# Sixteen more first products per layer, made beside the gate build and kept in DRAM

## The chip, the cores and the metric

The kernel runs on one core of one Trainium2 chip. The metric is device time in microseconds (us) of one execution; the time before is 4202.59 us, the median of three runs (4202.59 to 4206.1).

## The reference, cut to what matters

The model has two layers over 768 tokens (256 of a context, 512 latent) of width 1024. Each layer has a mixer (attention and the like) and then a PEER block: a router picks, for each token and each of 8 heads, 16 out of 16384 single-neuron experts. For a token `x`, the block gives the sum over its 128 picked experts of `gate * gelu(x . u[e]) * v[e]`:

```python
eidx = jnp.take_along_axis(cidx.reshape(n, PEER_HEADS, -1), ci, axis=-1)
gate = jax.nn.softmax(cs, axis=-1)
a = jnp.einsum('nd,nhkd->nhk', xt, u[eidx])
w = gate * jax.nn.gelu(a, approximate=False)
return jnp.einsum('nhk,nhkd->nd', w, v[eidx])
```

The second layer needs only the latent tokens.

## The kernel before, in words

**Dense and gathered tokens.** Of the 512 latent tokens of a layer, three blocks of 128 (`ND` = 384 tokens) are done densely: all 16384 experts are computed for them, and a matrix of gates that is zero for the experts not picked takes out the rest. The fourth block (and in the first layer the two context blocks) is done by gathering: one indirect DMA fetches one row of `u` or `v` for each of 128 tokens, VectorE multiplies it up. Such a step is called a row here (`gather`, L1010 to L1036). The rows are spread over other work by hand: 272 of the first layer's 768 lie in the mixer, 78 beside the gate build, 64 in the next mixer and the others in the dense loop; all 256 of the second layer lie in its dense loop.

**The order in one layer's `peer`.**

1. `route`: `scores` makes 16 query products (`pqps`) with weights that come through the buffers `wraw` (three), `whi` and `wlo` (two each) and the PSUM tag `pj` (two). Then `select` picks the experts of each block, nearly all on VectorE.
2. `gate_build`, once per dense block after that block's selection: 32 units per block, 96 per layer. A unit makes gates for four tokens: two matmuls `gds` (L1091), one VectorE operation (L1095) and one of ScalarE (L1097) on their result, then four fp32 matmuls `gps` (L1108, eight recorded pieces). Every second unit has a ScalarE copy to `gch`; every fourth stores 1 MB to `gd` in DRAM. `beside(hot)` is called once in each unit and places gathered rows, queued on VectorE behind the unit's L1095 (`issue_after` orders instructions of that one engine and no other's).
3. In the first layer only, `mod(1, [0, 1])`: 16 weight tiles through `wraw`, with results in `pj`.
4. The first products that are made early: for the first `UPRE` = 18 (second layer 27) groups of 128 experts, `dense_u` makes `z[j] = u_j . x` for 384 tokens. The weight tile (512 KB) comes through `wraw`, ScalarE casts it to `whi` (L195), GpSimd and VectorE in turn subtract to `wlo` (L196), 24 matmuls of 384 columns (L217) go to a `pj` tile, ScalarE copies to `z`.
5. The dense loop over 128 groups. Iteration `j` makes the first product of group `j + ahead` (24 matmuls L217; `ahead` is 21 and 28; weight tile `draw`, ScalarE cast L1122, GpSimd subtract L1123), turns `z[j+1]` into `w[j+1]` (`dense_w`: VectorE multiplies by the gates in L1168, ScalarE casts in L1171, VectorE subtracts in L1172), loads the second weight tile of group `j`, and adds its 18 matmuls of 512 columns (`dacc`, L1178). The `z` tiles form a ring of `ahead + 1` buffers. Rows are placed behind each iteration's L1172.

**What sets the order on each engine.** The order of each engine's instructions is fixed when the program is built, by a scheduler that plays the program against a model of its time. It takes, among the instructions that could start, the one that is written first; an instruction of a later step may go ahead as long as what is written earlier is not ready. A tile gets a buffer of its tag when one is free, and a tile that finds none waits. Loads of weights are issued on SP's queue.

Of the kernel before, what the change touches and what calls it, by code (L numbers as in the profile page):

```python
# [9 lines left out]
F32 = mybir.dt.float32  # L10
# [12 lines left out]
ND = 384  # L23
# [5 lines left out]
GROWS = 78, 0  # L29
# [2 lines left out]
NLAT = 5  # L32
FIRST = 1, 1, 0, 1, 0, 1, 0, 1, 0, 1, 0, 1, 1, 0, 0, 0
XA, VPRE = 2, 2
UEXT = 3, 1
TAIL = 4
GEND = 124
# [73 lines left out]
class Kern:  # L111
    def __init__(self, ctx, tc, a, dbg=None):
        self.ctx, self.tc, self.nc, self.a = ctx, tc, tc.nc, a
        self.dbg = dbg or {}
        E = ctx.enter_context
        self.pc = E(tc.tile_pool(name="cst", bufs=1, reuse_waits="tile"))
        self.pg = E(tc.tile_pool(name="gat", bufs=1, reuse_waits="tile"))
        self.px = self.xt = E(tc.tile_pool(name="xt", bufs=1, reuse_waits="tile"))
        self.dr = E(tc.tile_pool(name="dr", bufs=1, space=bass.MemoryType.DRAM))
        self.wk = None  # L120
        nc = self.nc
        self.tables()
        self.cst = self.pc.tile([128, CST_N], F32, name="cst")
        self.ident = self.c("ident")
        self.eps = self.pc.tile([128, 1], F32, name="eps")
        nc.vector.memset(self.eps, EPS)
        self.one = self.c("ones")[:, 0:1]
        self.modd = self.dr.tile([2, 2, 6 * D], F32, name="modd")
        self.hd = self.dr.tile([768, D], F32, name="hd")
        self.x2d = self.dr.tile([768, D], F32, name="x2d")  # L130
        self.h1 = self.dr.tile([768, D], F32, name="h1")
        self.gd = self.dr.tile([ND // 16, 128, 128, 16], F32, name="gd")
        self.yd = self.dr.tile([2, D, 768], F32, name="yd")
        self.bd = self.dr.tile([ND // 128, 1024, 256], BF16, name="bd")

    def consts(self):
# [979 lines left out]
    def halves(self, src, shape, eng):  # L1116
# [6 lines left out]
        eng.tensor_tensor(lo, raw, hi.bitcast(F32), op=OP.subtract)  # L1123
        return hi, lo

    def dense_u(self, j, u, A, xt):


        nc = self.nc
        self.proj2(A, u, xt, ND)  # L1130
        if j % (self.ahead + 1) <= self.upre:
            z = self.dz.tile([128, ND], F32, name="dz", tag="dz", bufs=self.upre + 1)
        else:
            z = self.dn.tile([128, ND], F32, name="dz", tag="dze", bufs=self.ahead - self.upre)
        if j < self.ahead:
            nc.scalar.copy(z, A)
        else:
            nc.scalar.activation(z, A, AF.Gelu)  # L1138
        return z
# [3 lines left out]
        return self.halves(self.a["pr_v"][r:r + 128, :], [D], self.nc.vector)  # L1143

    def ahead_u(self, l, n, pda, xt, z, eng):
        u = self.halves(self.a["uT"][l, n], [8, 128], eng)
        A = pda.tile([128, ND], F32, name="dA", tag="dA", bufs=2)
        z[n] = self.dense_u(n, u, A, xt)
# [10 lines left out]
    def dense_w(self, j, z):  # L1159
        nc = self.nc  # L1160
        JG = self.jg
        if j > 0 and j % JG == 0:
            self.load_gates(j, range(3))
        if j < self.ahead:
            with self.tc.issue_after(self.lastexp.ins):
                nc.scalar.activation(z, z, AF.Gelu)
        z3 = z.rearrange("p (c t) -> p c t", t=16)
        nc.vector.tensor_tensor(z3, z3, self.G[:, :, j % JG, :], op=OP.mult)  # L1168
        wh, wl = (self.dn.tile([128, ND], F32R, name="dw", tag="dw" + x, bufs=2) if j < 128 - TAIL else
                  self.dz.tile([128, ND], F32R, name="dw", tag="dz", bufs=self.upre + 1) for x in "hl")  # L1170
        nc.scalar.copy(wh, z)  # L1171
        i = nc.vector.tensor_tensor(wl, z, wh.bitcast(F32), op=OP.subtract)  # L1172
        return wh, wl, i
# [166 lines left out]
    def peer(self, l, xt, bb, gat, rows, done, late, put):  # L1340

        tc, nc = self.tc, self.nc
        PS = bass.MemoryType.PSUM
        nd = ND // 128
        nb = 4
        upre = self.upre = UPRE[l]
        self.ahead = upre + UEXT[l]
        self.jg = JGS[l]  # L1350
        with tc.tile_pool(name="dz", bufs=1, reuse_waits="tile") as self.dz:
            with self.mixing(), self.phase("rt"):
                pool, tag = ((self.wk, "sel"), (self.pg, "uv"))[l]
                alloc = lambda: pool.tile([128, D], F32, name="sel", tag=tag, bufs=5)
                self.gate_consts()
                step = [0]

                def beside(hot):

                    step[0] += 1  # L1360
                    if step[0] * GROWS[l] // 96 > (step[0] - 1) * GROWS[l] // 96:
                        with tc.issue_after(hot.ins):
                            next(rows)

                sel = self.route(l, xt, nb, nd, alloc, lambda *a: self.gate_build(*a, beside))
                if l == 0:
                    self.mod(1, [0, 1])
                z = {}
                for j in range(upre):
                    u = self.parts(self.weight(self.a["uT"][l, j], [128, 8, 128]), (nc.gpsimd, nc.vector)[j % 2])  # L1370
                    z[j] = self.dense_u(j, u, self.pj([128, ND], "dA"), xt)
            gat += [(bb + b, LAT, sel[b]) for b in range(nd, nb)]
            left, done = 256 * len(gat) - done - GROWS[l] - late, 0
            with tc.tile_pool(name="dn", bufs=1, reuse_waits="tile") as self.dn, \
                    tc.tile_pool(name="pda", bufs=1, space=PS, reuse_waits="tile") as pda, \
                    self.phase("d2"), tc.tile_pool(name="pd", bufs=1, space=PS, reuse_waits="tile") as pd:
                acc = [pd.tile([128, 2, 512], F32, name="dacc%d" % b) for b in range(nd)]
                self.load_gates(0, [0, 1])
                for n in range(upre, self.ahead):
                    self.ahead_u(l, n, pda, xt, z, (nc.gpsimd, nc.vector)[(n - upre) % XA])  # L1380
                vs = {n: self.v_rows(l, n) for n in range(VPRE)}
                self.load_gates(0, [2])
                w = {0: self.dense_w(0, z.pop(0))}
                last = []
                for j in range(128):
                    if j + self.ahead < 128:
                        self.ahead_u(l, j + self.ahead, pda, xt, z, nc.gpsimd)
                    if j == TJ:
                        self.tables(True)
                    if j + 1 < 128:  # L1390
                        w[j + 1] = self.dense_w(j + 1, z.pop(j + 1))
                    wj = w.pop(j)
                    v = vs.pop(j) if j in vs else self.v_rows(l, j)
                    if j < 128 - TAIL:
                        for b in range(nd):
                            self.dense_v(j, b, wj, v, acc)
                    else:
                        last.append((j, wj, v))
                    with tc.issue_after(wj[2].ins):
                        while done < min(left * (j + 2) // GEND, left):  # L1400
                            next(rows)
                            done += 1
                for b in range(nd):
                    for j, wj, v in last:
                        self.dense_v(j, b, wj, v, acc)
                m5 = self.row5(l, LAT)
                for b in range(nd):
                    put(bb + b, self.resid(m5, acc[b].rearrange("p h d -> p (h d)"), bb + b))
# [139 lines left out]
```

## Time and profile before

| | before |
| --- | --- |
| median of the runs shown | 4202.59 us |
| the profiled execution: its time, and its span | 4207.51 us, 4205.7 us |
| PE busy, PE weight loads busy | 3816.9 us (91%), 3259.6 us (78%) |
| VectorE (DVE) busy | 3316.6 us (79%) |
| ScalarE (ACT) busy | 1508.1 us (36%) |
| GpSimd (POOL) busy | 2261.8 us (54%) |
| mean granted clock of TensorE | 0.955 |

Times inside the profile count from the first instruction. The first layer's selection and gate build lie at about 1086 to 1390 us and its dense loop at about 1419 to 2400 us; the second layer's at about 2966 to 3240 us and 3247 to 4195 us. A busy time of PE is that of pipelined matmuls whose ends are modelled, so two views of it are needed: how often a matmul starts, and what lies in the gaps.

### The profile page before, as it was taken

How to read it: one execution, taken by the hardware profiler on the slowest of the kernel's cores; microseconds unless marked ns; L12 is line 12 of the kernel's file. 1: busy time of each engine (PE TensorE's matmuls, PEld its weight loads, DVE VectorE, ACT ScalarE, POOL GpSimd, SP SyncE). 2: the span in 40 equal slices, each digit the busy share in tenths (PEclk: the TensorE clock that was granted, in tenths of full speed). 3: DMA queues.
4: the chain of work that ended last, by engine and by line, in shares of the span. 5: the costliest groups of instructions: out<-in, count | busy, mean ns of one | idle time of the engine just before them, and what ended most of it. 6: DMA issues, size and time to landing. Idle time of an engine off the chain costs nothing.

```text
span 4205.7 us, 56328 instructions
## 1 busy us (share of the span) xinstructions
PE 3816.9 (91%) x19774; PEld 3259.6 (78%) x19780; DVE 3316.6 (79%) x5835; ACT 1508.1 (36%) x2746; POOL 2261.8 (54%) x1644
## 2 busy tenths in 40 slices
PE   8988776769888799999999889999989999999999
PEld 5776554547777699988999767777877899999987
DVE  4359888866998899989999987537875977777788
ACT  3322322312146333333333324332356333333333
POOL 1016777542454587877888563004531666666664
PEclk9999888879999999999999999999999999999999
DMA  5556898783449999999999995423346988787878
GB/s 192 172 200 209 308 322 307 253 287 121 149 161 398 367 332 334 332 324 333 346 339 331 341 333 194 158 85 111 111 160 235 346 279 285 275 290 273 282 268 313
DMA packets 389674, 1099.30 MB, mean 261 GB/s; under 512 B 32959, under 2 KB 140807, under 8 KB 383246
## 3 DMA queue, kind: packets, MB, share of 16 engines
q0 software_dynamic: 147456, 536.94, 35.2%
q1 hardware_dynamic: 232142, 497.95, 34.6%
q10 hardware_dynamic: 9792, 60.82, 3.5%
q8 instruction: 155, 2.54, 0.2%
q14 instruction: 129, 1.06, 0.1%
HBM read 1024.18 MB, written 71.40 MB: 260 GB/s over the span
## 4 chain that ended last, share of the span: by engine, by line
PE 58%; DVE 16%; DMA 11%; issue 8%; POOL 6%; ACT 2%; SPq 0%; ACTq 0%; POOLq 0%; DVEq 0%
PE dacc L1178 20%; PE dA L217 18%; POOL uv L1010 4%; DMA uv<-in_pr_u_dram,ix 3%; PE ops L223 3%; DMA uv<-in_pr_v_dram,ix 3%; PE pqps L217 2%; DVE junkv L1023 2%; PE gps L1108 2%; DMA draw<-in_uT_dram 1%; PE oo L1335 1%; DVE pacc L1036 1%; PE gds L1091 1%; PE modps L252 1%; PE oqps L210 1%
## 5 line engine op out<-in xcount | busy, mean ns | idle before, releaser
L1178 PE MATMUL dacc<-dhi,dw 128*128 128x512 f32 x3072 | 983.7, 390 | 3.4 <-ACT dw L1171 1.9
L1010 POOL DMA_INDIRECT uv<-in_pr_u_dram,ix x512 | 669.4, 1307 | 447.7 <-DVE pa L1023 316.0
L1010 POOL DMA_INDIRECT uv<-in_pr_v_dram,ix x512 | 680.0, 1328 | 408.0 <-DVE pacc L1036 281.9
L1023 DVE CUSTOM_DVE_ANT_0 junkv<-uv,x 128x1024 bf16<-128x1024 f32 x512 | 692.6, 1353 | 65.0 <-DMA uv<-in_pr_u_dram,ix 60.9
L1036 DVE SCALAR_TENSOR_TENSOR pacc<-uv,pw,pacc 128x1024 f32<-128x1024 f32 x508 | 701.5, 1381 | 39.3 <-DMA uv<-in_pr_v_dram,ix 35.4
L1178 PEld LDWEIGHTS dacc<-dhi,dw 128*128 128x128 f32 x3072 | 576.5, 188 | 119.5 <-ACT dw L1171 2.2
L1123 POOL TENSOR_TENSOR dlo<-draw,dhi 128x1024 fp32r<-128x1024 f32 x210 | 545.0, 2596 | 194.9 <-ACT dhi L1122 191.4
L1122 ACT CAST dhi<-draw 128x1024 fp32r<-128x1024 f32 x467 | 489.0, 1050 | 404.9 <-issue 179.5
L1178 PE MATMUL dacc<-dlo,dw 128*128 128x512 f32 x1536 | 601.6, 392 | 5.2 <-DVE dlo L1123 5.2
L1168 DVE TENSOR_TENSOR dz<-dz,dG 128x384 f32<-128x384 f32 x256 | 416.9, 1642 | 73.6 <-ACT dz L1138 71.8
L1171 ACT CAST dw<-dz 128x384 fp32r<-128x384 f32 x256 | 131.5, 514 | 721.2 <-PE dacc L1178 694.3
L1123 DVE TENSOR_TENSOR dlo<-draw,dhi 128x1024 fp32r<-128x1024 f32 x257 | 331.9, 1292 | 17.7 <-ACT dhi L1122 16.1
L217 PE MATMUL dA<-xth,dlo 128*128 128x384 f32 x1688 | 328.1, 335 | 19.0 <-POOL dlo L1123 19.0
L217 PE MATMUL dA<-xth,dhi 128*128 128x384 f32 x1688 | 334.6, 340 | 5.1 <-ACT dhi L1122 5.1
L1178 PEld LDWEIGHTS dacc<-dlo,dw 128*128 128x128 f32 x1536 | 288.2, 188 | 63.8 <-DVE dlo L1123 7.6
L217 PE MATMUL dA<-xtl,dhi 128*128 128x384 f32 x1688 | 326.9, 334 | 0.0
L217 PEld LDWEIGHTS dA<-xth,dhi 128*128 128x128 f32 x1688 | 305.7, 189 | 21.6 <-ACT dhi L1122 5.5
L217 PEld LDWEIGHTS dA<-xth,dlo 128*128 128x128 f32 x1688 | 296.5, 188 | 20.0 <-POOL dlo L1123 20.0
L217 PEld LDWEIGHTS dA<-xtl,dhi 128*128 128x128 f32 x1688 | 296.4, 188 | 0.0
L1172 DVE TENSOR_TENSOR dw<-dz,dw 128x384 fp32r<-128x384 f32 x256 | 154.4, 603 | 150.3 <-ACT dw L1171 150.3
L196 POOL TENSOR_TENSOR wlo<-wraw,whi 128x1024 fp32r<-128x1024 f32 x55 | 132.8, 2416 | 246.7 <-ACT whi L195 129.6
L1108 PEld LDWEIGHTS gps<-ghot 128*128 128x128 f32 x1536 | 205.0, 195 | 70.7 <-issue 39.0
(339 smaller groups left out, 6072.2 us busy)
## 6 DMA issues: line engine op xcount, KB each, us to landing
draw<-in_pr_v_dram SPq DMA_DIRECT2D x256, 512.0 KB
draw<-in_uT_dram SPq DMA_DIRECT2D x211, 512.0 KB
wraw<-in_wb_dram SPq DMA_DIRECT2D x150, 512.0 KB
gd<-gch ACTq DMA_DIRECT2D x48, 1024.0 KB
dG<-gd SPq DMA_DIRECT2D x30, 1536.0 KB
wraw<-in_mod_t_dram SPq DMA_DIRECT2D x48, 512.0 KB
wraw<-in_uT_dram SPq DMA_DIRECT2D x45, 512.0 KB
wraw<-in_mod_w_dram SPq DMA_DIRECT2D x32, 512.0 KB
```

What stands on the lines that cost most here:

```text
L196: eng.tensor_tensor(lo, raw, hi.bitcast(F32), op=OP.subtract)
L217: self.nc.tensor.matmul(ps, w[wi][:, k, :], x[xi][:, k, 0:T], start=(i == 0), stop=(i == 23))
L1010: nc.gpsimd.indirect_dma_start(out=t, out_offset=None, in_=a[table], in_offset=bass.IndirectOffsetOnAxis(ap=ix[:, c:c + 1], axis=0))
L1023: nc.vector.tensor_tensor_reduce(out=junk, in0=u, in1=x, op0=OP.mult, op1=OP.add, scale=1.0, scalar=0.0, accum_out=A[:, c:c + 1])
L1036: nc.vector.scalar_tensor_tensor(acc, v, W[:, c:c + 1], acc, op0=OP.mult, op1=OP.add)
L1108: nc.tensor.matmul(ps[0][:, t0 % 8 + t, :], h[0][:, t, :], h[1][:, t, :], start=True, stop=True)
L1122: nc.scalar.copy(hi, raw)
L1123: eng.tensor_tensor(lo, raw, hi.bitcast(F32), op=OP.subtract)
L1168: nc.vector.tensor_tensor(z3, z3, self.G[:, :, j % JG, :], op=OP.mult)
L1171: nc.scalar.copy(wh, z)
L1172: i = nc.vector.tensor_tensor(wl, z, wh.bitcast(F32), op=OP.subtract)
L1178: self.nc.tensor.matmul(acc[b][:, h, :], w[wi][:, 128 * b:128 * b + 128], v[vi][:, 512 * h:512 * h + 512], start=(j == 0 and i == 0), stop ...
```

## The change

In each layer, the first products of 16 more groups of experts are taken out of the dense loop. The list `spill` names them: they are spread evenly over the groups from `ahead` on. Each is made by a new function `store_u(k)`, called from `beside` at every fifth unit of the gate build from the 21st on (units 21, 26, ..., 96): weight tile through `wraw`, cast, subtract (on GpSimd in the first layer, on VectorE in the second), 24 matmuls into a `pj` tile, a VectorE copy to SBUF, and a store of 192 KB to the new DRAM tile `zd`. In the dense loop, a spilled group loads its 192 KB from `zd` into its `z` tile on SP's queue in place of the 512 KB weight tile, the cast, the subtract, the 24 matmuls and the evacuation; its Gelu, before part of the evacuation, is taken from the tile in `dense_w`. The 78 gathered rows beside the first layer's gate build lie beside units 17 to 96 now, before beside all 96.

```diff
 XA, VPRE = 2, 2
+USP = 16, 16
 UEXT = 3, 1
...
+        self.zd = self.dr.tile([2, max(USP), 128, ND], F32, name="zd")
...
+    def z_tile(self, j):
+        if j % (self.ahead + 1) <= self.upre:
+            return self.dz.tile([128, ND], F32, name="dz", tag="dz", bufs=self.upre + 1)
+        return self.dn.tile([128, ND], F32, name="dz", tag="dze", bufs=self.ahead - self.upre)
...
     def ahead_u(self, l, n, pda, xt, z, eng):
+        if n in self.spill:
+            z[n] = self.z_tile(n)
+            self.nc.sync.dma_start(z[n], self.zd[l, self.spill.index(n)])
+            return
...
-        if j < self.ahead:
+        if j < self.ahead or j in self.spill:
             with self.tc.issue_after(self.lastexp.ins):
                 nc.scalar.activation(z, z, AF.Gelu)
...
+        self.spill = [self.ahead + (127 - self.ahead) * k // USP[l] for k in range(USP[l])]
...
+                def store_u(k):
+                    u = self.parts(self.weight(self.a["uT"][l, self.spill[k]], [128, 8, 128]),
+                                   (nc.gpsimd, nc.vector)[l])
+                    A = self.pj([128, ND], "dA")
+                    self.proj2(A, u, xt, ND)
+                    t = self.wk.tile([128, ND], F32, name="zs", tag="pq", bufs=2)
+                    nc.vector.tensor_copy(t, A)
+                    nc.sync.dma_start(self.zd[l, k], t)
+
                 def beside(hot):
                     step[0] += 1
-                    if step[0] * GROWS[l] // 96 > (step[0] - 1) * GROWS[l] // 96:
+                    u = step[0] - 16
+                    if u > 0 and u * GROWS[l] // 80 > (u - 1) * GROWS[l] // 80:
                         with tc.issue_after(hot.ins):
                             next(rows)
+                    if u > 0 and u * USP[l] // 80 > (u - 1) * USP[l] // 80:
+                        with tc.issue_after(hot.ins):
+                            store_u((u - 1) * USP[l] // 80)
```

## Rows read from the trace of the kernel before

**Rows 1.** The page: granted clock of TensorE in forty slices of the span.
```profile
PE   8988776769888799999999889999989999999999
PEclk9999888879999999999999999999999999999999
```
**Rows 2.** Busy time of each engine in the two dense loops (us, in brackets instructions).
```profile
core 0: us, PE busy (x) PEld busy (x) DVE busy (x) ACT busy (x) POOL busy (x), PEclk, DMA share, GB/s
1440.00:2376.00 936.00, 930.53 (x4664) 841.07 (x4663) 869.82 (x846) 340.95 (x458) 728.77 (x435) 1.00 0.93 334
...
3262.00:4150.00 888.00, 886.32 (x4434) 800.41 (x4433) 716.38 (x720) 322.24 (x433) 581.92 (x336) 1.00 0.83 292
```
**Rows 3.** Timeline of one second-layer iteration: start, duration, engine, line.
```profile
3607.37 1.48 PEld L217 LDWEIGHTS dA<-xth,dhi 128*128 128x128 f32 x8
...
3611.61 0.19 PEld L1178 LDWEIGHTS dacc<-dhi,dw 128*128 128x128 f32 x1
...
3615.68 1.48 PEld L217 LDWEIGHTS dA<-xth,dhi 128*128 128x128 f32 x8
```
**Rows 4.** The second layer's gate build by windows: early units, then the others.
```profile
3030.00:3112.00 82.00, 71.77 (x401) 66.89 (x401) 75.56 (x219) 39.43 (x69) 45.27 (x43) 0.92 0.32 109
3112.00:3240.00 128.00, 121.84 (x850) 99.04 (x851) 58.12 (x84) 92.05 (x133) 2.15 (x4) 1.00 0.58 221
```
**Rows 5.** Timeline of two units of that gate build.
```profile
3150.21 1.08 PEld L1108 LDWEIGHTS gps<-ghot 128*128 128x128 f32 x8
...
3151.37 0.76 PE L1091 MATMUL gds<-gB,gbits 128*128 128x512 bf16 x2
3151.76 1.07 PEld L1108 LDWEIGHTS gps<-ghot 128*128 128x128 f32 x8 [0.29 <-issue]
...
3152.86 0.59 PE L1091 MATMUL gds<-gB,gbits 128*128 128x512 bf16 x2
...
3153.08 1.08 PEld L1108 LDWEIGHTS gps<-ghot 128*128 128x128 f32 x8
```
**Rows 6.** The first layer: selection, gate build, start of the dense loop.
```profile
1086.00:1150.00 64.00, 54.54 (x402) 44.96 (x401) 56.85 (x241) 10.93 (x16) 27.70 (x22) 1.00 0.51 174
1150.00:1390.00 240.00, 202.34 (x1269) 170.32 (x1271) 216.38 (x488) 129.57 (x195) 114.14 (x117) 0.96 0.77 291
```
**Rows 7.** Early first products in the first and second layer: PE, PEld, ACT on `dA`.
```profile
1086.00:1150.00 64.00, 21.71 (x125) 21.71 (x126) 2.40 (x5) 1.00 0.51 174
1150.00:1254.00 104.00, 60.75 (x309) 55.27 (x307) 6.19 (x13) 0.90 0.45 156
...
2966.00:3030.00 64.00, 58.31 (x324) 57.33 (x323) 6.22 (x13) 0.97 0.36 119
3030.00:3112.00 82.00, 61.00 (x289) 55.31 (x289) 5.69 (x12) 0.92 0.32 109
3112.00:3240.00 128.00, 0.25 (x2) 0.20 (x2) 0.48 (x1) 1.00 0.58 221
```
**Rows 8.** SP's queue after the scores: weight loads of steps 3 and 4, first layer.
```profile
1063.37 0.33 SPq L250 DMA_DIRECT2D wraw<-in_mod_t_dram  x1
...
1121.63 0.35 SPq L250 DMA_DIRECT2D wraw<-in_mod_t_dram  x1
...
1122.39 1.69 SPq L187 DMA_DIRECT2D wraw<-in_uT_dram  x2
...
1150.06 0.33 SPq L1077 DMA_DIRECT2D bd<-sel  x1
```
**Rows 9.** SP's queue in the second layer, to the first unit's loads.
```profile
2943.99 77.29 SPq L187 DMA_DIRECT2D wraw<-in_uT_dram  x16
3021.95 0.33 SPq L1077 DMA_DIRECT2D bd<-sel  x1
3027.14 0.93 SPq L1088 DMA_DIRECT2D gbits<-bd  x2
```
**Rows 10.** PE's timeline where the two dense loops start (in brackets idle, releaser).
```profile
1385.07 2.17 PE L1108 MATMUL gps<-ghot 128*128 128x128 f32 x16
1389.78 2.93 PE L217 MATMUL dA<-xth,dhi 128*128 128x384 f32 x8 [2.54 <-ACT dhi L1122]
...
1413.60 2.93 PE L217 MATMUL dA<-xth,dlo 128*128 128x384 f32 x8 [17.91 <-POOL dlo L1123]
...
1419.04 0.39 PE L1178 MATMUL dacc<-dhi,dw 128*128 128x512 f32 x1
...
3236.10 1.16 PE L1108 MATMUL gps<-ghot 128*128 128x128 f32 x8 [0.28 <-ACT ghot L1097]
...
3247.44 0.50 PE L1178 MATMUL dacc<-dhi,dw 128*128 128x512 f32 x1 [1.88 <-ACT dw L1171]
```
**Rows 11.** First-layer dense loop: L1168 by duration (min, median, max in ns).
```profile
L1168 DVE TENSOR_TENSOR dz<-dz,dG x97: 543/2374/3000, 1499.6 to 2299.4; 128x384 f32<-128x384 f32 x97
```
**Rows 12.** SP's queue in the second dense loop: what its longest waits are for.
```profile
SPq L1119 <- DVE dlo L1123: 282.6, 70, 4.6
SPq L1119 <- POOL dlo L1123: 190.9, 63, 4.0
```

More of the change, by code (lines that the diff above doesn't have):

```diff
@@ L1130, in dense_u @@
         self.proj2(A, u, xt, ND)
[L1131 to L1134, printed above, removed]
+        z = self.z_tile(j)
         if j < self.ahead:
```

## The prediction

> **What bounds the kernel now.** I read the page first, then the windows of each stage, then the timeline inside a stage. The page says PE, VectorE and at times the DMA queues are all near full, and the granted clock is near the upper of its two levels (2.4 GHz) nearly everywhere [rows 1]; so what a stage is worth is read stage by stage. In both dense loops PE is busy in 99% to 100% of the window [rows 2]. In the second layer nothing else is near full (VectorE 716 of 888 us, DMA share 0.83). In the first layer VectorE has 870 of 936 us and the DMA share is 0.93: a faster PE meets them soon. One iteration shows PE's price [rows 3]: 24 weight loads of a first product run from 3607.37 to 3611.61, 4.24 us, the second product to 3615.68, 4.07 us, sum 8.31 us, with no gap.
>
> The gate build is the place to which the products go. In the second layer PE is busy 121.8 of 128 us there, with VectorE at 58 us and ScalarE at 92 us [rows 4]; two units take 2.87 us (3150.21 to 3153.08), 1.435 us each, and the only pause is one of 0.29 us per pair [rows 5]. In the first layer the gate build shares its time with selection and rows: VectorE 216 of 240 us, PE 202 [rows 6].
>
> The last reading decides the forecast: what PE does before the gate units are ready. Selection is VectorE's work, and PE fills that time with step 4's early products, which are written after the gate build but are ready sooner. From 2966 to 3030 us they take 58.3 of 64 us, to 3112 another 61.0 of 82, and then none is left [rows 7]. In the first layer PE makes step 3 and then step 4 in this time (54.5 of 64 us busy, then 60.8 us of products to 1254) [rows 6, 7].
>
> **The change part by part.** *Taken out of the dense loops:* 16 first products per layer, 16 x 4.24 = 68 us of PE each [rows 3]. In the second layer PE is the only bound, so all 68 us come back. In the first layer PE would need 930.5 - 68 = 863 us for the window. VectorE keeps its instructions; some get shorter, since L1168 takes 543 ns alone and 2374 ns in the median [rows 11], which I put down to GpSimd's subtract running beside it, and 16 of those go: 16 x 1.83 = 29 us, so 841 us of work. At 95% fullness (93% now [rows 2]) that is 885 us. DMA: 16 x (512 - 192) KB = 5 MB less of some 313 MB, 0.93 x 936 = 870 us becomes about 856 us of full queues. I take 885, a gain of 51 us; bounds 25 us (no shorter instructions and 93% to 96% fullness) and 68 us.
>
> *The loads of `z`* wait for a buffer of the ring that `dense_w` frees, and SP's later loads queue behind them. SP's ordinary waits there, for a `draw` buffer, reach 4.6 us without PE noticing [rows 12, 2], and the ring buffer needed is that of two iterations earlier; I take nothing, with a rival below. The Gelu is moved, not added. ScalarE loses a cast; it is busy 36% of these windows [rows 2].
>
> *Put into the gate build:* 16 x 4.24 = 68 us of PE per layer, and on VectorE a copy that no row shows; its nearest neighbour is the 0.69 us operation on 512 columns of PSUM (L1095) in the unit, so 0.3 to 0.69 us, taken as 0.5: 8 us per layer, on a VectorE that is at 90% in the first layer and 45% in the second [rows 4, 6]. In the second layer the subtracts add some 20 us to a VectorE that has 70 us free [rows 4]. Stores and loads of 192 KB are 3 MB a layer, 10 us of DMA at 291 GB/s [rows 6], hidden where the DMA share is under 0.8. The pauses of PE (0.29 us per pair, some 12 us over 85 units) could take a little of the 68; I take nothing.
>
> *What it moves.* `store_u` is written before steps 3 and 4 and needs the same buffers: `wraw`, `whi`, `wlo`, `pj`. Only its VectorE instructions are queued behind a unit; its weight load, cast and matmuls are not. So right after the scores the first three `store_u` take the three `wraw` buffers, two take `whi` and `pj`, and they hold them: a `pj` tile is freed by a VectorE copy that stands behind unit 21, 26 and so on. Each buffer that comes free goes to the next `store_u`, which is written earlier than step 3 or 4. The trace has the same contest: all 16 weight loads of step 3 were issued, the first at 1063.37 before the scores were done and the last at 1121.63, before the first of step 4 at 1122.39, though step 4 could have started as well [rows 8]. So steps 3 and 4 get no buffer until about unit 90 of 96. The PE work that filled the time of the selection goes behind the gate build, where nothing covers it.
>
> *Second layer.* After the scores PE has two `store_u` (their first 16 matmuls, 2 x 2.8 us) and then nothing until the first unit. That came when the gate bits were loaded at 3027, and the PE work at 3030 [rows 9, 4]. Without step 4's subtracts VectorE gets there some 10 us sooner: 3020. From there PE has 96 x 1.435 = 138 us of units, 68 - 6 = 62 us of `store_u`, 27 x 4.24 = 114 us of step 4, and about 10 us of pauses while selection and units share VectorE (as 82 - 71.8 now [rows 4]): 324 us, to 3344. The first `dacc` came 10.2 us after the last unit ended (3237.3 to 3247.4 [rows 10]); 3354 against 3247.4 is **+107 us**, with the loop's 68 us back **+39 us**.
>
> *First layer.* From 1086 PE has two `store_u` and then waits for the first unit, at about 1150. From there VectorE is the bound: 216.4 us [rows 6] less 11 us of step 4's subtracts plus 8 us of copies is 213.5, at the present 90% 237 us, to 1387, about where the gate build ends now. Then step 3 (PE was 29.7 us on it, the rest of 54.54 - 21.71 [rows 6, 7] being scores' remains) and 18 x 4.24 = 76 us of step 4: 106 us, to 1493. The start of the dense loop should be quicker: now PE waits 17.9 us for a weight tile while the queues carry rows [rows 10], and in a tail without rows it would not; I take 10 us as in the second layer. First `dacc` at 1503 against 1419: **+84 us**, with 51 us back **+33 us**.
>
> The sum is +72 us on the profiled execution's 4207.5 us, 4279.5; the runs' median is 4.9 us under it, so **4274 us**. Idle PE also costs clock: after its 17.9 us of idling the first eight matmuls took 2.93 us against about 1.6 [rows 10]; that is 1.3 us a time, inside the error. Bounds of this case: 4242 (first-layer loop gives all 68 us, gate build 15 us faster) to 4315 (it gives 25, and PE stands 15 us longer).
>
> **A rule weighed.** PE's busy share in the second layer's gate build is 95%, its weight loads' 99.0 of 128 us, 77% [rows 4]. The Trainium skill ("Perfetto Trace Analysis", section Identifying the Most-Contended Engine) says the share of weight loads, not of matmuls, tells PE's headroom: by that 29 us of products would fit into this stage at no cost, and the sum would be 21 us lower than by the 8 us of pauses that the first rival counts. The timeline speaks against it here: between the weight loads of two units lie the two 512-column `gds` matmuls [rows 5], which use the array and have short weights.
>
> **The rivals.** *1. Nothing is displaced* (the scheduler gives step 4 its buffers as before). Then the second layer only exchanges: +68 - 8 in the gate build, -68 in the loop, -8. In the first layer 80 units would be PE's at 1.435 + 4.24/5 = 2.28 us against 136 us / 80 = 1.70 now: +47; the 12 rows that now lie before 1254 leave a full VectorE, -16; loop -51: -20. Sum -28: **4175 us**. For it: PE's early work shows that later steps do overtake; against it [rows 8]. *2. Displaced in part*, so that the costs meet: about 28 of the 100 us lost to displacement would cancel the gain of rival 1: **4195 to 4211 us**. *3. SP's queue is held by the `z` loads* in the dense loops, without displacement. It decides once such a wait is longer than the two iterations (16 us) by which loads lead; if each of the 32 then costs PE the 4.24 us that it saved, rival 1 becomes 4175 + 119 = **4294 us**. Against it: PE's windows are full beside waits of 4.6 us.
>
> **How the numbers follow.** Displacement 0.64 (4274, own range 4242 to 4315), rival 1 0.21, rival 2 0.09, rival 3 0.06. The bound of what can be told from no change is 0.2%, 8.4 us. Slower 0.64 + 0.06 = 0.70, same 0.09, faster 0.21. The range must leave out no more than 0.2: from 4180, which cuts off a good half of rival 1 (0.12), to 4315 (0.06).
>
> **What would show it.** Right: PE nearly idle after the scores of each layer until the first `gds` (some 45 to 55 us), no early `dA` products of step 4 before the gate build's last units, 18 and 27 of them in a block after it with `modps` of step 3 among them in the first layer, the second dense loop about 68 us and the first about 50 us shorter. Wrong: step 4's weight loads issued between the scores and the first unit, as now; or a dense loop that does not shrink, with SP waiting on L1172 for a `z` load.

## The result and the profile after

The changed kernel takes 4349.98 us (median of 4 runs, 4347.23 to 4351.64) against 4203.68 us (4202.59 to 4206.1) for the kernel before in the same comparison: a ratio of 1.034, 95% interval 1.033 to 1.036. It is slower by 146 us. The prediction was slower by about 70, 4274 us with a range of 4180 to 4315. The measured time lies 35 us above that range: the direction was right, the size was about half.

The profiled execution spans 4347.4 us, 141.7 more than before. Five stretches add up to that, bar 1.0 us before the first. Each is cut at the first or last start of a group (`pqps` are the scores' products, `dacc` the second product of the dense loop, `hm` VectorE's first instruction on a finished `dacc`):

| stretch, us | before | after | difference |
|---|---|---|---|
| 1st layer: first `pqps` to first `dacc` (selection, gate build, steps 3 and 4) | 438.6 | 554.3 | +115.7 |
| 1st dense loop: first `dacc` to first `hm` | 989.7 | 982.7 | -7.0 |
| mixer: first `hm` to the second layer's first `pqps` | 441.5 | 430.1 | -11.4 |
| 2nd layer: first `pqps` to first `dacc` | 397.2 | 502.0 | +104.8 |
| 2nd dense loop: first to last `dacc` | 947.7 | 886.3 | -61.4 |

The page's slices, to be held against [rows 1], show a hole in PE ahead of each dense loop and another behind the first loop. The granted clock, full there before, falls with them: to 7 tenths in the slice of each hole ahead of a loop, to 8 in the two slices around the first loop's end.

```profile
PE   8988677669479999999999569998499999999999
PEclk9999888879799999999999889999799999999999
```

Windows of the stretches between the scores and the first gate unit, first and second layer. In the first, PE was busy 54.54 of 64 us before [rows 6]; the second is where step 4's products ran [rows 7]. Now PE stands, at 0.63 and 0.52 of the full clock in the mean, while VectorE selects:

```profile
1086.00:1150.00 64.00, 15.33 (x74) 13.04 (x74) 53.07 (x280) 5.15 (x9) 28.17 (x30) 0.63 0.14 50
3068.00:3115.00 47.00, 5.19 (x23) 3.47 (x24) 37.87 (x192) 2.83 (x7) 18.02 (x24) 0.52 0.07 23
```

SP's queue in the same kernel says why (start, duration, queue, line). The weight loads at 1076.50 are those of added products; the next one starts at 1203.56, in the gate build, and step 3's `mod_t` begins at 1348.41, where it began at 1063.37 before [rows 8].

```profile
1076.50 30.93 SPq L189 DMA_DIRECT2D wraw<-in_uT_dram  x6
...
1203.56 0.33 SPq L189 DMA_DIRECT2D wraw<-in_uT_dram  x1
...
1348.41 0.33 SPq L252 DMA_DIRECT2D wraw<-in_mod_t_dram  x1
...
1443.66 0.35 SPq L189 DMA_DIRECT2D wraw<-in_uT_dram  x1
...
3030.69 0.33 SPq L189 DMA_DIRECT2D wraw<-in_uT_dram  x1
...
3042.96 5.80 SPq L189 DMA_DIRECT2D wraw<-in_uT_dram  x2
3104.90 0.33 SPq L1079 DMA_DIRECT2D bd<-sel  x1
...
3333.33 88.67 SPq L189 DMA_DIRECT2D wraw<-in_uT_dram  x23
```

In the second layer SP loaded 16 weight tiles between 2943.99 and the gate bits before [rows 9]; now it gets three in there (3030.69 and 3042.96), and 23 in one go after the gate build. The tile `dA` by windows (PE, PEld, DVE, ACT), against [rows 7], shows the same from PE's side: in each layer step 4 is one solid block behind the gate build.

```profile
1086.00:1150.00 64.00, 10.58 (x48) 9.85 (x48) 0.00 (x0) 0.00 (x0) 0.63 0.14 50
1150.00:1254.00 104.00, 13.86 (x72) 12.44 (x72) 1.63 (x3) 0.00 (x0) 0.86 0.56 197
1447.00:1522.00 75.00, 73.76 (x424) 73.53 (x425) 0.00 (x0) 8.18 (x17) 1.00 0.42 137
3068.00:3115.00 47.00, 0.00 (x0) 0.00 (x0) 0.00 (x0) 0.00 (x0) 0.52 0.07 23
3333.00:3442.00 109.00, 108.12 (x624) 107.80 (x622) 0.00 (x0) 12.99 (x27) 1.00 0.42 138
```

The first dense loop has the other surprise. By the tiles `dacc` and `hm`, PE's part takes 917.5 us, 1535.7 to 2453.2, against 985.9 before: the 68 us are saved in full. But VectorE comes to the result only at 2518.4, 65 us after the last `dacc`; before it was 3.8 us. The loop before, and then after:

```profile
L1178 PE MATMUL dacc<-dhi,dw x1536: 387/389/496, 1419.0 to 2404.9; 128*128 128x512 f32 x192
...
L1052 DVE TENSOR_TENSOR hm<-dacc,m x3: 1219/1225/1225, 2408.7 to 2415.4; 128x1024 f32<-128x1024 f32 x3
```

```profile
L1186 PE MATMUL dacc<-dhi,dw x1536: 387/389/501, 1535.7 to 2453.2; 128*128 128x512 f32 x192
...
L1054 DVE TENSOR_TENSOR hm<-dacc,m x3: 1215/1218/1225, 2518.4 to 2523.1; 128x1024 f32<-128x1024 f32 x3
```

The windows of this loop, of those 60 us behind it and of the second loop (columns as in [rows 2]):

```profile
1535.00:2453.00 918.00, 912.87 (x4516) 817.30 (x4516) 846.68 (x869) 337.64 (x462) 686.22 (x413) 1.00 0.93 338
2455.00:2515.00 60.00, 1.97 (x8) 1.57 (x8) 45.62 (x45) 3.30 (x8) 35.00 (x28) 0.53 0.93 343
3475.00:4280.00 805.00, 801.63 (x3962) 719.15 (x3962) 657.89 (x691) 295.75 (x406) 547.73 (x312) 1.00 0.86 305
```

In the 60 us PE does nothing, and the DMA share is the same 0.93 as in the loop: token rows that are written ahead of the loop's result are still being fetched (15.1 of the 20.6 MB moved there; most of the rest is loaded for the mixer). The second loop is PE's alone (801.63 of 805 us), as before.

### The profile page after: what moved, and what is told of

The parts are those of the page before. It is cut to its first block, busy times and chain, and to the rows that moved or that the text cites. A ratio compares the mean times of both kernels' runs of the same rounds, so it can differ in the third digit from the quotient of the medians.

```text
span 4347.4 us, 56448 instructions
## 1 busy us (share of the span) xinstructions
PE 3818.7 (88%) x19780; PEld 3257.9 (75%) x19780; DVE 3255.5 (75%) x5883; ACT 1514.8 (35%) x2746; POOL 2235.0 (51%) x1628
## 4 chain that ended last, share of the span: by engine, by line
PE 56%; DVE 16%; DMA 12%; issue 9%; POOL 5%; ACT 1%; SPq 0%; ACTq 0%; POOLq 0%; DVEq 0%
PE dA L219 19%; PE dacc L1186 17%; DMA uv<-in_pr_v_dram,ix 4%; POOL uv L1012 3%; PE ops L225 3%; DMA uv<-in_pr_u_dram,ix 3%; PE pqps L219 2%; PE gps L1110 2%; DVE junkv L1025 2%; DVE pacc L1038 2%; PE modps L254 1%; PE gds L1093 1%; PE oo L1343 1%; DMA draw<-in_uT_dram 1%; DVE sel L979 1%
## 5 line engine op out<-in xcount | busy, mean ns | idle before, releaser
L1025 DVE CUSTOM_DVE_ANT_0 junkv<-uv,x 128x1024 bf16<-128x1024 f32 x512 | 727.8, 1421 | 62.3 <-DMA uv<-in_pr_u_dram,ix 57.5
L1125 POOL TENSOR_TENSOR dlo<-draw,dhi 128x1024 fp32r<-128x1024 f32 x178 | 467.7, 2628 | 146.7 <-ACT dhi L1124 86.7
L198 POOL TENSOR_TENSOR wlo<-wraw,whi 128x1024 fp32r<-128x1024 f32 x71 | 169.3, 2386 | 525.3 <-PE dA L219 245.0
L1176 DVE TENSOR_TENSOR dz<-dz,dG 128x384 f32<-128x384 f32 x256 | 266.7, 1058 | 56.6 <-ACT dz L1174 28.3
L219 PE MATMUL dA<-xth,dhi 128*128 128x384 f32 x1432 | 283.4, 340 | 5.4 <-ACT dhi L1124 5.4
L219 PE MATMUL dA<-xtl,dhi 128*128 128x384 f32 x1432 | 278.7, 335 | 0.0
L219 PE MATMUL dA<-xth,dlo 128*128 128x384 f32 x1432 | 277.1, 334 | 0.0
L219 PEld LDWEIGHTS dA<-xth,dhi 128*128 128x128 f32 x1432 | 258.7, 189 | 20.2 <-ACT dhi L1124 6.5
L219 PEld LDWEIGHTS dA<-xtl,dhi 128*128 128x128 f32 x1432 | 252.7, 189 | 0.0
L219 PEld LDWEIGHTS dA<-xth,dlo 128*128 128x128 f32 x1432 | 251.0, 188 | 0.4
```

The costliest lines, as they stand in the source:

```text
L219: self.nc.tensor.matmul(ps, w[wi][:, k, :], x[xi][:, k, 0:T], start=(i == 0), stop=(i == 23))
L1025: nc.vector.tensor_tensor_reduce(out=junk, in0=u, in1=x, op0=OP.mult, op1=OP.add, scale=1.0, scalar=0.0, accum_out=A[:, c:c + 1])
```

## The experiments

All kernels but two were timed in several rounds against the kernel before; the stretches are those of the table above, in its order, from the profiled execution of each. x9 and x10 leave out work of the first mixer's rows too (their first `pqps` comes at 924 and 932 us, in the changed kernel at 981), so only their stretches are to be compared, not their times.

| run | median us | ratio to before (95%) | stretches, us |
|---|---|---|---|
| x1_order | 4250.8 | 1.009 to 1.012 | 492.6, 988.9, 427.8, 466.4, 884.7 |
| x2_second | 4249.2 | 1.008 to 1.013 | 435.2, 994.8, 440.6, 502.3, 883.3 |
| x3_rows | 4212.4 | 0.999 to 1.002 | 425.9, 1017.8, 431.7, 394.9, 947.6 |
| x4_late96 | 4332.9 | 1.029 to 1.033 | 556.0, 920.1, 479.1, 503.1, 885.4 |
| x5_unused | 4421.5 | 1.048 to 1.051 | 553.4, 995.9, 440.6, 502.2, 946.5 |
| x6_constant | 4141.9 | 0.983 to 0.986 | 426.0, 1015.3, 426.4, 399.3, 883.0 |
| x7_second_order | 4213.3 | 1.000 to 1.002 | 437.7, 989.8, 442.2, 466.5, 886.3 |
| x8_order_late96 | 4236.3 | 1.004 to 1.008 | 491.5, 926.2, 476.9, 467.5, 883.8 |
| x9_half_vector | 4240.9 (one run) | | 536.5, 965.6, 417.5, 500.9, 883.9 |
| x10_half_fetch | 4243.6 (one run) | | 552.6, 916.6, 442.6, 501.4, 886.4 |

**The order alone.** Step 3 and step 4 (18 products in the first layer, 27 in the second) are taken from their old place behind `route` (not shown) and written ahead of the first added product, at a lower priority, so that they come first in the use of `wraw`, `whi`, `wlo` and `pj`:

```diff
+                z = {}
+                def early():
+                    with self.later():
+                        if l == 0:
+                            self.mod(1, [0, 1])
+                        for j in range(upre):
+                            u = self.parts(self.weight(self.a["uT"][l, j], [128, 8, 128]), (nc.gpsimd, nc.vector)[j % 2])
+                            z[j] = self.dense_u(j, u, self.pj([128, ND], "dA"), xt)
...
+                    if u == 1:
+                        early()
                     if u > 0 and u * USP[l] // 80 > (u - 1) * USP[l] // 80:
                         with tc.issue_after(hot.ins):
                             store_u((u - 1) * USP[l] // 80)
```

> All 32 added products stay, and so do their stores and reads; only the place in the program is changed: the modulation products of the next layer and the 18 (second layer: 16) products of the gate build are written before the first added product, as their users of the same buffers, so that they get weight buffers, the SP queue and PE first. Displacement theory (the added products cost what the earlier work loses by coming after them): PE is busy again in the stretch that was idle (1086 to 1150 us, and 3068 to 3115), the first dacc comes at 1430 to 1460 us instead of 1535, the second layer's gate build and step 4 take 400 to 430 us instead of 502, the second loop keeps its 886 us; the first loop stays near 983 us, as its end is set by the token rows. Sum: 4204 + (10 to 40) - 7 - 11 + (3 to 33) - 61, so 4140 to 4200, taken as 4180. Rival (the products cost their own time beside the gate units, wherever the other work stands): little changes, 4320 to 4350.

Measured: 4250.8 us, against 4349.98 for the changed kernel. So about 100 of the 146 us were the displacement, and they come back by order alone: PE is busy 54.38 of the 64 us from 1086 to 1150, and the two starts are 62 and 36 us earlier than in the changed kernel. But the rest of the expectation failed: the time is 51 us above the upper end of 4200. Beside the first kernel the two starts are still 54 and 69 us later. So the products are not hidden beside the gate units even when nothing is displaced. The window of the second layer's gate build from the point where step 4's early products end:

```profile
3150.00:3333.00 183.00, 182.06 (x1220) 160.60 (x1219) 79.39 (x112) 102.83 (x143) 2.26 (x1) 1.00 0.51 189
```

PE has 182.06 of 183 us: there is no room. In the timeline one product (here its first 16 matmuls) simply pushes the next unit away: 4.1 us from `gds` to `gds`, where the units next to it follow one another at 1.3 to 1.4 us.

```profile
3205.50 0.61 PE L1093 MATMUL gds<-gB,gbits 128*128 128x512 bf16 x2
3205.95 1.05 PE L1110 MATMUL gps<-ghot 128*128 128x128 f32 x8
3206.76 1.64 PE L219 MATMUL dA<-xth,whi 128*128 128x384 f32 x8
3208.24 1.55 PE L219 MATMUL dA<-xtl,whi 128*128 128x384 f32 x8
3209.63 0.61 PE L1093 MATMUL gds<-gB,gbits 128*128 128x512 bf16 x2
3210.07 1.05 PE L1110 MATMUL gps<-ghot 128*128 128x128 f32 x8
```

**One layer, and the order in that layer.** x2 has `USP = 0, 16` and the rows as before the change; x7 is the same with x1's order.

```diff
-USP = 16, 16
+USP = 0, 16
...
-                    if u > 0 and u * GROWS[l] // 80 > (u - 1) * GROWS[l] // 80:
+                    if step[0] * GROWS[l] // 96 > (step[0] - 1) * GROWS[l] // 96:
```

> Only the second layer has the 16 added products; the first layer is as it was before the change, its rows beside the gate units too. If the two layers' costs add as the stages show them: 4204 + 105 - 61 = 4248 (4240 to 4256), so 99 us of the 146 belong to the first layer. Rival (the loss is the first layer's alone, and the second's later start is only a consequence of what the first pushes ahead of it): 4180 to 4215.

> The order of x1 with added products in the second layer alone. TensorE was found busy 182 of 183 us in x1's second gate build after the first units, so a product there costs what it saves in the loop. Theory (TensorE bounds both places): 4204 + 69 - 63 = 4210, 4203 to 4217. Rival (what was lost in x1's second layer came from its first): 4175 to 4195.

x2 came within 2 us of the sum that was expected: the layers' costs add, and the first layer has about 100 of the 146 us. x7 gives back all but 5 us of the second layer's loss, and cannot be told from the kernel before: +69 us ahead of the loop, -61 in it. Both places are full of PE's work, so what was carried from one to the other was worth nothing there.

**The rows' place alone.** `USP = 0, 0`, with the rows beside units 17 to 96:

> No added product at all; only the rows that stand beside the gate units are spread over units 17 to 96 instead of 1 to 96, as in the change. Theory: the shift is next to nothing, 4200 to 4212. Rival (the rows are what moved the end of the first gate build to 1411 us and left 32 rows over at the end of the first loop): 4220 to 4240.

It is the same within what can be measured, at the upper edge of what was expected. The stretches are worth a look all the same: the loop starts 13 us sooner and takes 28 us more, with 30 us of rows left after the last `dacc`. Between the scores and the first `dacc` there are 65 rows where there were 78: the other 13 have moved into the loop.

**More rows to the mixer.** x4 is the changed kernel, x8 is x1, each with `LATE = 96` instead of 64, and nothing else edited:

> The changed kernel, but 32 token rows more are kept out of the first dense loop and left to the next mixer (96 instead of 64). Row theory (in the first loop it is the rows, not TensorE, that set the end, so the 51 us are made but not given back): the stretch from the first dacc to the first row of the loop's result falls from 983 us to 920 to 935, the mixer takes 0 to 25 us more, time 4295 to 4325. Rival (the loop is held by the chain from z to dacc): the stretch stays at 975 to 985, time 4345 to 4370.

> x1 with 96 instead of 64 token rows left to the next mixer. Theory (rows are a bound of the whole first layer and of the mixer behind it, so they cost about the same wherever they stand): the first loop ends 65 to 70 us sooner, the mixer takes 45 to 50 more, 4251 - 18 = 4233, 4225 to 4242. Rival (the mixer has room once the loop ends in time, and x4's 49 us came from elsewhere): 4180 to 4205, which would beat the kernel before.

The tiles of x4's first loop: the result is now read 0.3 us after the last `dacc`.

```profile
L1186 PE MATMUL dacc<-dhi,dw x1536: 387/389/628, 1532.4 to 2452.2; 128*128 128x512 f32 x192
...
L1054 DVE TENSOR_TENSOR hm<-dacc,m x3: 1212/1216/1216, 2452.5 to 2457.6; 128x1024 f32<-128x1024 f32 x3
```

So the loop was held by the rows, as the row theory has it: 63 us gone with 32 rows. What it got wrong is the mixer, which takes 49 us more, not 0 to 25; of the 63 us only about 14 stay, and the median falls by 17 us, to a little above the expected range. x8 shows the same pair again (-63, where 65 to 70 were expected, and +49), its time as expected. It is not the version that beats the kernel before: it is still slower by 0.4% to 0.8%.

**Price and gain apart.** In x5 the products are made and stored and never read; `ahead_u` makes each of them in the loop again, with its Gelu where it was before the change. In x6 nothing is made: a constant tile is stored for each product, and the loops read it. First x5's edit, in `ahead_u`,

```diff
-        if n in self.spill:
-            z[n] = self.z_tile(n)
-            self.nc.sync.dma_start(z[n], self.zd[l, self.spill.index(n)])
-            return
```

and x6, in `store_u`:

```diff
-                    u = self.parts(self.weight(self.a["uT"][l, self.spill[k]], [128, 8, 128]),
-                                   (nc.gpsimd, nc.vector)[l])
-                    A = self.pj([128, ND], "dA")
-                    self.proj2(A, u, xt, ND)
                     t = self.wk.tile([128, ND], F32, name="zs", tag="pq", bufs=2)
-                    nc.vector.tensor_copy(t, A)
+                    nc.gpsimd.memset(t, 0.5)
```

> The 32 products are made and stored beside the gate units as in the change, but never read: the dense loops make all their first products themselves, as before the change. It shows the price alone. If price and gain add: 4204 + 117 + 105 = 4426, less up to 11 in the mixer, so 4412 to 4430; the first loop lasts 985 to 992 us to its result's first row, the second 947. Rival (part of the later start is made up in the loops by work that waits there, whatever the loops hold): 4370 to 4400.

> The 32 products are left out: a constant tile is stored in place of each, and the loops read it where they read the product. No weight is loaded and TensorE does nothing for them, so it shows the gain alone, the most that moving these products could ever bring. Theory (first loop set by the rows, second by TensorE): the first layer gains 0 to 18, the second 61 to 64, time 4122 to 4145. Rival (the first loop would gain its 51 to 68 us if it started on time): 4070 to 4095.

Both times are as expected; x5's first loop, 995.9 us, is 4 us longer than that. The price alone is 4421.5 - 4207.9 = 214 us, the gain alone 4207.9 - 4141.9 = 66 us; the difference, 148, is the change's 146. The gain is the second layer's: there 947.7 becomes 883.0. In x6's first layer PE's work is gone from the loop at no cost, and its three stretches sum to 1867.7 us against 1869.8 before. Its rows lie as in x3, 13 more of them in the loop than before; x3's three stretches sum to 1875.4 us, so the products' absence is worth 8 us beside that, which is less than single executions of one kernel differ. The last `dacc` starts at 2330.8 and the result waits for rows until 2418.8, where it was 2408.7 before:

```profile
L1186 PE MATMUL dacc<-dhi,dw x1536: 387/389/628, 1403.5 to 2330.8; 128*128 128x512 f32 x192
...
L1054 DVE TENSOR_TENSOR hm<-dacc,m x3: 1214/1217/1223, 2418.8 to 2423.5; 128x1024 f32<-128x1024 f32 x3
```

**What holds the rows.** The changed kernel with half of VectorE's work per row in the first layer (x9), and with half of the fetches (x10):

```diff
-                nc.vector.tensor_tensor_reduce(out=junk, in0=u, in1=x, op0=OP.mult, op1=OP.add,
+                n = D // 2 if l == 0 else D
+                nc.vector.tensor_tensor_reduce(out=junk[:, 0:n], in0=u[:, 0:n], in1=x[:, 0:n], op0=OP.mult, op1=OP.add,
```

```diff
-                u = fetch("pr_u", ix, c)
+                if l == 1 or c % 2 == 0:
+                    u = fetch("pr_u", ix, c)
```

and each the same for the rows of v.

> The changed kernel with half of VectorE's work on each token row of the first layer: the two row operations take 512 of the 1024 columns, the other half of the columns is left out; all rows are still fetched whole. It asks what holds the rows in the first loop (in the changed kernel 65 us of rows are left after the last dacc, and the last unit of the gate build starts 259 us after the first). If VectorE holds them: first dacc to the first row of the result 915 to 925 us, gate build 225 to 240. If the fetches hold them (transfers, their issue by GpSimd, five buffers): 965 to 985 us, gate build 250 to 260.

> The changed kernel with half of the token rows' fetches in the first layer left out: each fetched row is used for two columns of the gates, so VectorE's work is whole and the other half of the rows is left out of the sum. If VectorE holds the rows in the first loop: 970 to 985 us from the first dacc to the first row of the result, gate build 250 to 260. If the fetches hold them: 915 to 925 us, gate build 225 to 240. If the loop needs both: each of the two kernels falls part of the way.

Windows inside the first loop, x9 and then x10:

```profile
1480.00:2390.00 910.00, 893.68 (x4421) 800.89 (x4420) 650.64 (x855) 333.55 (x457) 595.80 (x417) 0.99 0.94 342
```

```profile
1480.00:2390.00 910.00, 903.44 (x4476) 809.05 (x4475) 877.75 (x893) 337.73 (x465) 506.84 (x263) 1.00 0.76 256
```

With VectorE relieved (651 of 910 us) the loop still takes 965.6 us, 17 less than in the changed kernel, and leaves 55 us of rows; with half the fetches it takes 916.6 and leaves none, though VectorE is then busier, 878 of 910 us. So in the loop the rows are held by what hangs on the fetches more than by VectorE's work on them, at a DMA share of 0.94. Each is a single run, but the two lie 49 us apart. What it is about the fetches is not shown: the transfers, their issue by GpSimd, the five buffers, or the order of VectorE's queue, which the scheduler lays down with the fetches in its model. For the transfers speaks that the bytes moved hardly differ (below); against them alone, that in x9's window VectorE stood only 14.3 us for a row's transfer, while GpSimd waited longer for VectorE to free a row's buffer:

```profile
DVE pacc L1039 <- DMA uv<-in_pr_v_dram,ix: 14.3, 12, 2.3
...
POOL uv L1012 <- DVE pacc L1039: 99.3, 53, 7.8
```

The gate build answers the other way. Its `gds`, in the changed kernel, x9 and x6:

```profile
L1093 PE MATMUL gds<-gB,gbits x192: 376/379/634, 1148.8 to 1408.1; 128*128 128x512 bf16 x192
...
L1094 PE MATMUL gds<-gB,gbits x190: 376/379/634, 1090.4 to 1326.9; 128*128 128x512 bf16 x190
...
L1093 PE MATMUL gds<-gB,gbits x189: 376/377/391, 1150.7 to 1370.3; 128*128 128x512 bf16 x189
```

They run over 259.3 us in the changed kernel, 236.5 with VectorE relieved, and 264.8 with half the fetches (above both ranges that were expected of x10). There VectorE is part of the limit and the fetches are not.

## Why the prediction was wrong about the first layer

The sum was +72 us, the profiled executions differ by 141.7. Of the 70 us between, 44 are the first loop's gain that did not come (the mixer gives back 11 of them), 33 are the first layer's later start, and 4 are the second layer's.

**Displacement: right.** The weight buffers went to the added products, PE stood between the scores and the gate units, and steps 3 and 4 came behind the gate build as blocks. x1 undoes it by order alone and gets about 100 us back.

**Second layer: right.** Start +105 us (+107 forecast), loop -61 (-68). Step 4's block took 109 us (114). Together +43 against +39. Some of that is luck: the first unit came 18 us sooner, not 10, and from there to the end of step 4 it took 331 us, not 324. Of the 7 us missing in the loop, 3 are pauses of PE (5.5 us against 2.0); the rest was not taken apart.

**First layer, "with 51 us back": this term failed.** The loop gave 7 us, and the mixer behind it another 11. The step that failed is the choice of the bound. The prediction saw that "a faster PE meets them soon", took VectorE as the one it meets, and let the transfers off with "870 us becomes about 856 us of full queues". But that is 856 us at a share of 1; at the 0.93 that the loop had [rows 2] it is 920 of the 936 us, a gain of 16 us. The later of the two ends counts, so 16 was the sum to take, under the lower bound of 25 that was given. That bound does not follow from its own condition either: 870 us of VectorE's work at 93% fullness is 936 us, no gain. VectorE's term itself came near: its busy time fell by 24 us, 29 were set. The 2374 ns behind it, though, are the median of 97 instructions from 1500 to 2300 us; over the whole loop the median of 121 is 554 ns, and that GpSimd's subtract makes the long ones long is not shown. The bytes agree with a bound by the transfers. Before, in a window of this loop from its first `dacc` to its first `hm`:

```profile
1419.00:2409.00 990.00, 980.44 (x4898) 883.76 (x4896) 919.04 (x900) 354.50 (x476) 762.31 (x457) 1.00 0.93 334
```

and after:

```profile
1535.00:2518.00 983.00, 915.43 (x4525) 819.04 (x4524) 895.17 (x915) 340.94 (x470) 722.29 (x443) 0.97 0.93 338
```

990 us x 334 GB/s is 331 MB, 983 x 338 is 332 MB: the same load at nearly the same rate. The 5 MB that were to be saved do not show in these sums. x6 shows that even for free the first layer would have gained 2 us, or 8 beside x3. x10 shows that with fewer fetches PE's 68 us do arrive in the loop. The loop before had PE and the rows ending within 4 us of each other, so both had to become cheaper.

**First layer, "+84 us": mis-sized, with a step that failed.** It measured +117 (first `dacc` 1535.7 against 1419.0). Step 3, step 4 and the start took some 124 us where 116 were set. The larger part is the end of the gate build, 1411 instead of 1387. The step that failed here is that VectorE, "at the present 90%", sets that end and the products lie beside it. x6's gate build, without products, has its `gds` over 219.6 us, the changed kernel's over 259.3: 40 us for products that were to cost VectorE's 8 us of copies. VectorE fell to 85% of the window (220.3 of 259 us). PE and VectorE take turns within a unit, and a product of some 4 us lies between them; that they alternate is argued from the timeline, not shown by a run.

**The rival "nothing is displaced", 4175 us: its condition was made in x1, its price failed.** It gave the second layer -8 and measured +6; it gave the first -20 and measured +40 (1909.3 - 1869.8): +54 ahead of the loop where it had +47 - 16 = +31, and -1 in the loop for its -51, with the mixer giving back 14. So the better order did not win either: in the second layer it is PE for PE, in the first it is PE for nothing. PE stood 27 of the 397 us before the second loop in the kernel before; no order that fills those pauses was tried.

**The rule weighed.** By weight loads' share there would have been 29 us of free room in the second layer's gate build. The measurement decides against it: with nothing displaced (x1 and x7) the loop's start moved by 69 us, all of the 16 x 4.24 = 68 us of PE that went there, at a weight loads' share of 160.60 of 183 us in x1. Here the Trainium skill ("Perfetto Trace Analysis", section Identifying the Most-Contended Engine) would have misled by its weight loads' share, and matmul busy share with the timeline did not. The section names the model FLOPs utilisation (MFU) beside that share; it was not worked out here.

**SP held by the reads of `z`: not seen.** SP waits up to 8.9 us for `draw` buffers in the second loop, no wait on the load of `z` is among its listed ones, and PE is busy 801.63 of 805 us beside them. What did wait for the loads is ScalarE's Gelu: 43.1 us in the second loop, ten times, up to 7.4 us. The rival's own sum was uneven: its +119 us are the two loops' gains, 68 + 51, while 32 times 4.24 is 136. VectorE's copies `zs` took 549 ns in the median, 0.5 us forecast.

**Open.** The mixer takes 10 to 24 us less wherever rows are left over at the end of the first loop (after, x1, x3, x6, and x9, whose rows there cost VectorE half), and 441 to 443 us where none are, but for the runs with 96 rows. What of it moves into that gap was not tried. Why 32 rows cost the mixer 49 us was not taken apart either.

## What to carry to other kernels

Before work is moved from a full loop into a stage, sum PE's busy time over that stage after its early part too: a stage at 95% (121.84 of 128 us [rows 4]) was no cover here, and an even exchange was the best that came of it. With this scheduler new users of a shared ring of buffers take it in the order in which they are written, so filler work that was free because it ran early must stay written ahead of them. And where two streams end a loop within a few us of each other, cost each by its own bound at the share it really reaches (here transfers at 0.93), and take the later; a gain on the one alone was worth 2 to 8 us of 68 here.

## Not expected of the hardware

The mean rate of the transfers in the first loop hardly moved: 334 GB/s before, 338 after, 342 with VectorE relieved, each at a share of 0.93 to 0.94; and it was 343 in the 60 us behind the loop, in which PE did next to nothing. That looks like a ceiling, but the 60 us are not alike inside. Two windows of the changed kernel:

```profile
2453.00:2469.00 16.00, 0.59 (x3) 0.17 (x1) 10.63 (x15) 3.30 (x8) 7.58 (x8) 0.66 1.02 412
2477.00:2485.00 8.00, 0.00 (x0) 0.00 (x0) 7.35 (x6) 0.00 (x0) 5.58 (x5) 0.50 0.76 258
```

Right behind the loop the same queues moved 412 GB/s, rows and the mixer's weights and other tiles together. So 334 to 343 GB/s is what this loop's mix reached and no limit of the chip, and whether PE's or VectorE's traffic takes anything from it stays open.
